# A decoder-layer kernel on one core: the row part of the mLSTM runs as a generator of its own in the second column block of each half

## The chip, the core and the metric

The kernel runs on one core of a Trainium2 chip. The core's engines each take their instructions in order: TensorE (PE in the profile; its weight loads are PEld), VectorE (DVE), ScalarE (ACT), GpSimd (POOL), and SyncE (SP), which in this kernel issues the DMAs. They wait for one another by semaphores. The metric is the time of one execution on the device in microseconds; the kernel before has a median of 2633.44 us over three runs (2632.45 to 2636.21).

## The reference

One layer of a hybrid decoder over 2048 positions of width 1024. A projection feeds three groups of heads: forgetting attention (8 heads), an mLSTM matrix memory (4 heads) and a spatial gating unit (SGU). Cut to what matters here:

```python
p = h @ w_in        # h = RMSNorm(x) * (1 + scale1) + shift1, from mod = silu(c) @ W_ada + b_ada
(q_a, k_a, v_a, q_m, k_m, v_m, o_m, u_s, v_s, f_a, i_m, f_m) = split(p)
F = cumsum(log_sigmoid(f_a))                       # bias of the attention's logits
# mLSTM, chunk by chunk, with the state C, n, m carried on
logf = log_sigmoid(f_m);  bcum = cumsum(logf)
m_t = max(bcum + m, max_s(bcum_t - bcum_s + i_s))
w_intra = exp(bcum_t - bcum_s + i_s - m_t);  w_inter = exp(bcum + m - m_t)
sc = (q k^T) * w_intra
num = w_inter * (q C) + sc v;  den = w_inter * (q n) + sum(sc)
h_out = num / max(|den|, exp(-m_t))
C_new = decay * C + sum_s w_state_s k_s v_s
y_mlstm = sigmoid(o_m) * rms_norm(h_out, g_m_out)
x = x + gate1 * (concat(y_attn, y_mlstm, y_sgu) @ w_out)   # then the ConvFFN
```

The gates' rows (`logf`, `i`, the running maximum `m`, the cumulative sums) are short: 4 heads by 2048 positions. From them come the column factors by which the mLSTM's products are scaled.

## The kernel before

The kernel has a projection stage, then attention, the output projection and the ConvFFN. Only the projection stage (to about 760 us) is touched. It goes twice through seven column blocks of `w_in`, once for each half of the sequence (1024 positions): `steps = [(half, i) ...]`. The blocks of a half are, in order: k of the mLSTM with the gates (`use_km`, i = 0), q and o of the mLSTM with the second half of v's columns (`do_qo`, i = 1), v of the mLSTM (`use_vm`, i = 2), the SGU (`use_sgu`, i = 3), and k, q and v of the attention (`use_qk`, `use_qk`, `use_v`, i = 4 to 6). What the text calls the second block is i = 1.

A block has 8 groups, each one accumulator (`acc`, three of them in PSUM) filled by 24 matmuls: 8 slices of the contraction by the three products `wh hh`, `wl hh`, `wh hl` (L54 to L56), since operands are split into a rounded high and a low part. Then the group is evicted: by ScalarE in `do_qo` (`evq`, L680 and L683) and in `use_km` (L658), by VectorE in `use_vm` (`ev`, L688), by both in `use_qk` (`qsq` on ScalarE, L765, statistics on VectorE, L767, `qn`, L773, and after the transposes `qhi` on ScalarE and `qlo` on VectorE, L786). `use_sgu` has `sy` (L733, L734) and its transposes (L741). The weights of the next block are loaded (`wr`, L582) and split (`wh` by ScalarE, L592; `wl` by VectorE, L593) during a block.

After each group, and in `do_qo` and the other 512-wide blocks once more after its fourth slice, a tick is called. A tick runs callbacks that are due (`after(n, f)`), then one step of each list: `chores`, which in the first half has `rest_of_mod` (each step loads a 128 x 512 piece `wa` of `w_ada` two pieces ahead and adds it into `modacc`, L466 and L468; after eight pieces a row is added, L474), and `background`, whose first generator runs to its next `yield`. So the order in the text is an interleaving by ticks. Each engine's final order comes from a scheduler and may differ from the text, but within an engine it is fixed and executed in order.

`mlstm(qi)` (L852) handles 512 positions, two of them a half. It starts with the row part: the gates are transposed into `psG` (L862, PSUM buffers `mps`), then a chain of VectorE instructions on four rows of 512 (L867 to L887): two scans, the differences, the tile `R` of four row groups (cleared by a memset, L877), `dec`, and a bf16 split of a row in `neb`. The next step makes the attention's cumulative sums `fr` (L891) and stores them to `nf_d`. Three yields later `R` is transposed back (`psR`, L903), and `ecol`, `acol` and `dcol` (L906 to L913) hold the column factors. The rest works per chunk of 128 positions and ends with `yt` (L1038), the mLSTM's output, which is stored to `yt_d`. `yt` shares the tag `sq` (two buffers) with `evq` and `qsq`; `fr` shares `macc` (two) with `modacc`. Tiles of one tag share its buffers: a new one waits until the users of the old one in its buffer are done, stores included.

`mlstm(2*half)` joins `background` in block i = 2 after its fourth group (L690), `mlstm(2*half + 1)` after that block. `log_gates(half)` (L796 to L806) turns the gates into logarithms, two activations (Exp, Ln) with their table loads between four VectorE instructions; the text calls it after block i = 1.

Of the kernel before, what the change touches and what calls it, by code (L numbers as in the profile page):

```python
# [8 lines left out]
F32 = mybir.dt.float32  # L9
F32R = mybir.dt.float32r  # L10
BF16 = mybir.dt.bfloat16
AF = mybir.ActivationFunctionType
ALU = mybir.AluOpType
# [4 lines left out]
P = 128  # L18
# [15 lines left out]
def trunk(  # L34
# [7 lines left out]
    V, A, G, T = nc.vector, nc.scalar, nc.gpsimd, nc.tensor  # L42
# [82 lines left out]
    pool, pp = Mem(), Mem(PSUM)  # L125
# [219 lines left out]
    def down_open_right():  # L345
# [8 lines left out]
        ("wr", 2048, 4), ("wh", 2048, 12), ("wl", 2048, 12), ("st", 8, 4), ("ss", 32, 4),  # L354
    )
    pool.open(
        "proj_r", "right", ("t4k", 4096, 5), ("t2k", 2048, 4), ("macc", 2048, 2), ("sq", 2048, 2), ("tmpA", 512, 2), ("lg", 512, 2), ("fc", 4, 1),
        ("mu", 16, 4), ("wT", 2048, 1), ("gsgu", 1024, 1), ("gbias", 64, 1), ("maskT", 1024, 1),
        ("rmask", 2048, 1), ("sel", 1024, 1), ("selb", 1024, 1), ("neb", 1024, 1), ("dec", 16, 1), ("qz", 2048, 2), ("Cst", 1040, 1), ("mcar", 4, 1), ("ra", 2048, 1), ("rb", 2048, 1),
        ("R", 2048, 1), ("mprev", 20, 2), ("ecol", 1088, 2), ("acol", 64, 2), ("dcol", 32, 2),  # L360
        ("qT", 1024, 2), ("kn", 1024, 2), ("v1", 1040, 2), ("H", 4160, 1), ("kT", 1024, 2), ("M1", 2048, 2),
        ("sc", 2048, 2), ("tm", 1040, 1), ("kw", 1024, 2), ("den", 64, 2), ("nd", 64, 2), ("mss", 64, 2),
# [12 lines left out]
    def misc_ps():  # L375
        return pp.tile([P, 512], F32, name="mp", tag="mp")

    def mps():
        return pp.tile([P, 512], F32, name="mps", tag="mps")
# [241 lines left out]
    background = []  # L621
# [174 lines left out]
    def log_gates(half):  # L796

        g = gates[:, half].rearrange("p a n h -> p (a n h)")
        mn = pool.tile([P, P], F32, name="lg0", tag="lg")
        ab = pool.tile([P, P], F32, name="lg1", tag="lg")  # L800
        V.tensor_scalar(mn, g, 0.0, None, op0=ALU.min)
        V.scalar_tensor_tensor(ab, mn, 2.0, g, op0=ALU.mult, op1=ALU.subtract)
        A.activation(ab, ab, AF.Exp)
        A.activation(ab, ab, AF.Ln, bias=1.0)
        V.tensor_tensor(g[:, 0:64], ab[:, 0:64], mn[:, 0:64], op=ALU.subtract)
        V.tensor_tensor(g[:, 96:P], mn[:, 96:P], ab[:, 96:P], op=ALU.subtract)  # L806


    fc = pool.tile([36, 1], F32, name="fc")
    V.memset(fc, 0.0)  # L810

    rmask = pool.tile([68, 512], F32, name="rmask")[64:68]
# [3 lines left out]
    V.memset(selb, 0.0)  # L816
    for r in (32, 64, 96):
        V.tensor_copy(selb[r : r + 4], bc(ident[r : r + 4, r : r + 4], 2, P))
    neb = pool.tile([P, 512], BF16, name="neb")
    V.memset(neb, 0.0)  # L820

    qzs = [pool.tile([P, 2, 2, P], F32, name="qz%d" % i, tag="qz") for i in range(2)]
    for t in qzs:
# [25 lines left out]
    mcar = pool.tile([68, 1], F32, name="mcar")[64:68]  # L849
    V.memset(mcar, 0.0)  # L850

    def mlstm(qi):  # L852
        t0 = qi * 512
        ra = pool.tile([P, 512], F32, name="ra", tag="ra")
        rb = pool.tile([P, 512], F32, name="rb", tag="rb")
        r4 = lambda t: t.rearrange("p (n l) -> p n l", l=P)
# [4 lines left out]
            o = (qi % 2 * 4 + i) * 4  # L861
            T.transpose(psG[0:100, i * P : (i + 1) * P], g[:, o : o + 100], ident)  # L862
        psI = psG[64:68, :]

        m, e, lf = ra[0:4], ra[32:36], ra[64:68]
        b, a, ne = rb[0:4], rb[32:36], rb[64:68]
        V.tensor_copy(lf, psG[96:100, :])  # L867
        mp_ = pool.tile([36, 5], F32, name="mprev", tag="mprev")[32:36]
        V.tensor_copy(mp_[:, 0:1], mcar)
        V.tensor_tensor_scan(m, lf, psI, mcar, op0=ALU.add, op1=ALU.max)  # L870
        V.tensor_tensor_scan(b, rmask, lf, 0.0, op0=ALU.mult, op1=ALU.add)
        V.tensor_tensor(a, psI, b, op=ALU.subtract)
        V.tensor_tensor(e, m, b, op=ALU.subtract)
        V.tensor_copy(mp_[:, 1:5], r4(m)[:, :, P - 1])
        V.tensor_copy(mcar, mp_[:, 4:5])
        R = pool.tile([P, 512], F32, name="R", tag="R")
        V.memset(R, 0.0)  # L877
        V.tensor_tensor(r4(R[0:4]), bc(mp_[:, 0:4], 2, P), r4(e), op=ALU.subtract)
        V.tensor_scalar(R[32:36], m, -1.0, None, op0=ALU.mult)
        V.tensor_tensor(r4(R[64:68]), r4(a), r4(e)[:, :, P - 1 : P].broadcast_to([4, 4, P]), op=ALU.subtract)  # L880
        V.tensor_copy(R[96:100], a)
        V.tensor_tensor(dec[0:4], mp_[:, 0:4], r4(e)[:, :, P - 1], op=ALU.subtract)

        V.tensor_scalar(neb[32:36], e, -1.0, None, op0=ALU.mult)
        V.scalar_tensor_tensor(ne, e, -1.0, neb[32:36], op0=ALU.mult, op1=ALU.subtract)
        V.tensor_copy(neb[64:68], ne)
        V.tensor_tensor(neb[96:100], ne, neb[64:68], op=ALU.subtract)  # L887
        yield
        fr = pool.tile([P, 512], F32, name="fr", tag="macc")
        for r in (0, 32):  # L890
# [4 lines left out]
            V.tensor_copy(fc[r : r + 4], fr[r : r + 4, 511:512])  # L895
            dma(nf_d[r // 8 : r // 8 + 4, t0 : t0 + 512], fr[r : r + 4])
        yield
        yield
        yield

        psR = mps()
        for i in range(4):
            T.transpose(psR[:, i * P : i * P + 100], R[0:100, i * P : (i + 1) * P], ident[0:100, 0:100])  # L903
        psR4 = psR.rearrange("p (n l) -> p n l", l=P)
        ecol = pool.tile([P, 4, 68], F32, name="ecol", tag="ecol")
        A.activation(ecol, psR4[:, :, 0:68], AF.Exp)  # L906
        acol = pool.tile([P, 4, 4], F32, name="acol", tag="acol")
        V.tensor_copy(acol, psR4[:, :, 96:100])
        psD = mps()
        for pr in range(2):  # L910
            T.matmul(psD[:, pr * 4 : pr * 4 + 4], sel[:, pr, :], dec, start=True, stop=True)
        dcol = pool.tile([P, 2, 4], F32, name="dcol", tag="dcol")
        A.activation(dcol.rearrange("p a b -> p (a b)"), psD[:, 0:8], AF.Exp)  # L913

        H = pool.tile([P, 4, 4, 65], F32, name="H", tag="H")

        got = {}
# [115 lines left out]
        for j in range(2):  # L1033
            yp = mps()
            for n in range(4):
                T.transpose(yp[:, n * P : (n + 1) * P], hq2[:, n, j * P : (j + 1) * P], ident)
            yt = pool.tile([P, 512], F32, name="yt", tag="sq")
            V.scalar_tensor_tensor(yt, yp, gmo[:, j : j + 1], om[:, j, :], op0=ALU.mult, op1=ALU.mult)  # L1038
            dma(yt_d[512 + j * P : 640 + j * P, t0 : t0 + 512], yt)

# [19 lines left out]
    for n, (half, i) in enumerate(steps):  # L1060
        if i == 0:
            make_h(half * 2, x0)
            if half == 0:
                head_setup()
            make_h(half * 2 + 1)
        elif n == nb - 1:
            x0 = [load_x(8 + t) for t in range(4)]
        if n == len(steps) - 1:
            while background:
                if next(background[0], True):  # L1070
                    background.pop(0)
            n_accs[0] = 2
            pool.close("proj_r")
            pp.close("proj_r")
            attention_open_right()

            load_k(0)
            first_rows = [], []
            first = [scores(0, tb, load_q(0, tb, "qA"), r) for tb, r in zip((1, 0), first_rows)]
            load_v(0, (0, 1))  # L1080
            background += first
        nxt[0] = Weights(blocks[steps[n + 1][1]][0]) if n + 1 < len(steps) else None
        blocks[i][1](half, cur)
        started.append(n)
        if nxt[0]:
            nxt[0].cast()
        cur = nxt[0]
        if i == 1:
            log_gates(half)
        if i == 2:  # L1090
            background.append(mlstm(half * 2 + 1))
        if n == nb + 2:
            small_setup()
# [76 lines left out]
    class Block:  # L1170
# [7 lines left out]
        def rows(self, i):  # L1178
            return slice(self.tb * TB + i * P, self.tb * TB + i * P + P)
# [544 lines left out]
```

## Time and profile before

| | us |
|---|---|
| median of 3 runs | 2633.44 (2632.45 to 2636.21) |
| the profiled execution's span | 2631.3 |
| projection stage, first half: second block (i = 1) | 79.0 to 123.6 |
| projection stage, second half: second block | 425.0 to 468.7 |
| TensorE's idle time between 70 and 760, sum | 30.6 |

The median lies 2.1 us above the span of the profiled execution. A row of the timeline has the start and the length in us, the engine, the line, the operation, the tiles written and read with partitions x elements, and in brackets the engine's idle time before it and what ended that. A row of the waits has the waiting engine with tile and line, the arrow to what it waited for, and total us, number and longest.

### The profile page before, as it was taken

To read this page: it belongs to the slowest core of one execution; us is meant where nothing else is said; L and a number is where in the kernel's file an instruction comes from. 1 tells how busy PE (TensorE), PEld (TensorE's weight loads), DVE (VectorE), ACT (ScalarE), POOL (GpSimd) and SP (SyncE) were. 2 spreads that over 40 slices of the span, in tenths; PEclk is the share of its full clock that TensorE was granted. 3 is DMA by queue.
4 is the path that set the end of the run, shared out by engine and by line. 5 is a ranking of instruction groups with operands and counts; after the bars stand their busy time and mean duration, and the time that the engine had idled before them with its cause. 6 is when DMAs were issued, how large, how long until landed. Compare 5 with 4: busy or idle time off the path is not lost.

```text
span 2631.3 us, 36459 instructions
## 1 busy us (share of the span) xinstructions
PE 2539.3 (97%) x12537; PEld 2103.0 (80%) x12537; DVE 2007.0 (76%) x3440; ACT 1269.2 (48%) x2420; POOL 398.9 (15%) x532
## 2 busy tenths in 40 slices
PE   5998999989999999999989999999999999999999
PEld 4886888878787887777868888888888888888787
DVE  7577743565368888866769888888888887898797
ACT  4333343333268888853555444544444444444443
POOL 2012210122336665630000000000000000000000
PEclk9999999999999999999999999999999999999999
DMA  7744653334564355247723222246222226648523
GB/s 244 227 135 131 195 163 107 109 88 121 164 176 116 106 146 149 78 153 238 275 76 104 81 88 80 89 145 232 88 88 81 80 72 247 237 162 302 185 96 116
DMA packets 302592, 379.58 MB, mean 144 GB/s; under 512 B 31934, under 2 KB 194588, under 8 KB 300360
## 3 DMA queue, kind: packets, MB, share of 16 engines
q1 hardware_dynamic: 302408, 377.26, 44.7%
q8 instruction: 99, 1.62, 0.2%
q14 instruction: 85, 0.70, 0.1%
HBM read 276.44 MB, written 100.74 MB: 143 GB/s over the span
## 4 chain that ended last, share of the span: by engine, by line
PE 79%; DVE 11%; DMA 4%; issue 2%; ACT 2%; POOL 1%; SPq 0%; DVEq 0%; ACTq 0%; POOLq 0%
PE ub L56 10%; PE ub L54 10%; PE ub L55 10%; PE acc L54 6%; PE acc L56 6%; PE acc L55 6%; PE db L55 4%; PE db L56 4%; PE db L54 4%; PE sp L206 4%; PE tp L259 3%; PE op L245 2%; PE op L246 2%; DVE wspl L1468 2%; PE wps L56 2%
## 5 line engine op out<-in xcount | busy, mean ns | idle before, releaser
L54 PE MATMUL acc<-wh,hh 128*128 128x512 f32 (+2 forms) x768 | 289.2, 378 | 8.5 <-DVE ev L688 6.6
L54 PE MATMUL ub<-T,wsph 128*128 128x512 f32 x704 | 274.2, 390 | 5.8 <-ACT wsph L1336 5.8
L56 PE MATMUL acc<-wh,hl 128*128 128x512 f32 (+2 forms) x768 | 277.3, 364 | 0.3 <-DVE hl L563 0.3
L55 PE MATMUL acc<-wl,hh 128*128 128x512 f32 (+2 forms) x768 | 277.2, 363 | 0.0
L56 PE MATMUL ub<-T,wspl 128*128 128x512 f32 x704 | 273.7, 389 | 1.7 <-DVE wspl L1337 1.7
L55 PE MATMUL ub<-T,wsph 128*128 128x512 f32 x704 | 273.9, 389 | 0.0
L55 PE MATMUL db<-wspl,wsph 128*128 128x512 f32 x616 | 240.3, 390 | 2.0 <-DVE wspl L1468 1.9
L56 PE MATMUL db<-wsph,wspl 128*128 128x512 f32 x616 | 239.6, 389 | 0.0
L54 PE MATMUL db<-wsph 128*128 128x512 f32 x616 | 238.3, 389 | 0.3 <-ACT wsph L1467 0.3
L1336 ACT CAST wsph<-S 128x512 fp32r<-128x512 f32 x176 | 109.7, 623 | 227.2 <-PE ub L55 157.4
L263 DVE TENSOR_TENSOR plo<-tp,phi 128x512 fp32r<-128x512 f32 (+1 forms) x320 | 186.9, 607 | 31.3 <-ACT phi L262 29.1
L54 PE MATMUL ub<-B,wsph 128*128 128x512 f32 x528 | 207.4, 393 | 2.8 <-ACT wsph L1336 2.8
L56 PE MATMUL ub<-B,wspl 128*128 128x512 f32 x528 | 206.9, 392 | 0.3 <-DVE wspl L1337 0.3
L55 PE MATMUL ub<-B,wsph 128*128 128x512 f32 x528 | 207.0, 392 | 0.0
L223 ACT ACTIVATE L<-L,nm 128x1024 f32<-128x1024 f32 (+2 forms) x192 | 172.6, 902 | 36.0 <-DVE nm L212 34.6
L262 ACT CAST phi<-tp 128x512 fp32r<-128x512 f32 (+1 forms) x320 | 160.0, 521 | 41.1 <-PE tp L259 39.5
L259 PE MATMUL tp<-ident,L 128*128 128x128 f32 x1088 | 177.2, 275 | 2.7 <-POOL L L228 0.9
L206 PE MATMUL sp<-kk,q 128*128 128x512 f32 (+3 forms) x640 | 170.0, 377 | 3.3 <-DVE nm L212 2.2
L54 PEld LDWEIGHTS acc<-wh,hh 128*128 128x128 f32 x768 | 148.3, 193 | 27.9 <-DVE ev L688 6.9
L228 POOL TENSOR_SCALAR L<-L,rs 128x1024 f32<-128x1024 f32 (+2 forms) x192 | 167.3, 881 | 11.0
L1467 ACT CAST wsph<-act 128x512 fp32r<-128x512 f32 x132 | 82.2, 623 | 179.3 <-PE db L55 162.5
L56 PEld LDWEIGHTS acc<-wh,hl 128*128 128x128 f32 x768 | 147.2, 193 | 23.0 <-DVE hl L563 0.8
(340 smaller groups left out, 5934.0 us busy)
## 6 DMA issues: line engine op xcount, KB each, us to landing
w<-in_w_up_dram SPq DMA_DIRECT2D x88, 512.0 KB
wd<-in_w_down_dram SPq DMA_DIRECT2D x176, 256.0 KB
wa<-in_w_ada_dram SPq DMA_DIRECT2D x96, 256.0 KB
act_d<-yc SPq DMA_DIRECT2D x44, 512.0 KB
act<-act_d SPq DMA_DIRECT2D x44, 512.0 KB
wr<-in_w_in_dram SPq DMA_DIRECT2D x64, 256.0 KB
q<-q_d SPq DMA_DIRECT2D x128, 128.0 KB
hc_d<-hl SPq DMA_DIRECT2D x28, 512.0 KB
```

The costliest lines, as they stand in the source:

```text
L54: T.matmul(ps, lh, rh, start=start, stop=False, skip_group_check=resume)
L55: T.matmul(ps, lh, rl, start=False, stop=False, skip_group_check=resume)
L56: T.matmul(ps, ll, rh, start=False, stop=stop, skip_group_check=resume)
L206: T.matmul(sp[:, b : b + bw], q2[n][:, qs], kk[:, s0 + b : s0 + b + bw], start=n == 0, stop=n == 1 and not last)
L223: A.activation(L[c], L[c], AF.Exp, bias=nm[:, n - 1 : n], scale=-1.0, accum_out=rs[:, c : c + 1])
L228: G.tensor_scalar(t, t, rs[:, 0:1], 1.0, op0=ALU.mult, op1=ALU.mult)
L245: T.matmul(op[:, c0:], vv[:, j, :], hi[:, c0:], start=(j == 0), stop=False)
L259: T.transpose(tp[:, i * P : (i + 1) * P], rows[i][j // 8][:, (j % 8) * P : (j % 8 + 1) * P], ident)
L262: A.copy(hi[:, c0:], tp[:, c0:])
L263: V.tensor_tensor(lo[:, c0:], tp[:, c0:], hi[:, c0:].bitcast(F32), op=ALU.subtract)
L1336: A.copy(hi, src)
L1467: A.copy(hi, v)
```

## The change

The row part of `mlstm` becomes a generator `rows(qi)` with steps of its own. Both generators of a half join `background` behind block i = 0, where `log_gates` is now called too, so that they run in block i = 1 one after the other: the gate transposes with the first copies; the two scans; the differences and half of `R`; the rest of `R` and `dec`; `fr`; the transposes back with `psD` (now in a buffer of `misc_ps` instead of `mps`) and the first half of `neb`; and the column factors with the rest of `neb`. `cols[qi]` hands the factors to `mlstm`, which starts with two empty steps. `neb` has two buffers, `R` one that is cleared once at the start. `log_gates` uses the tag `tmpA` instead of `lg`, which is dropped. `yt` takes the buffers `ra` and `rb` instead of `sq`.

```diff
--- before.py
+++ after.py
@@ -354,9 +354,9 @@
         ("wr", 2048, 4), ("wh", 2048, 12), ("wl", 2048, 12), ("st", 8, 4), ("ss", 32, 4),
     )
     pool.open(
-        "proj_r", "right", ("t4k", 4096, 5), ("t2k", 2048, 4), ("macc", 2048, 2), ("sq", 2048, 2), ("tmpA", 512, 2), ("lg", 512, 2), ("fc", 4, 1),
+        "proj_r", "right", ("t4k", 4096, 5), ("t2k", 2048, 4), ("macc", 2048, 2), ("sq", 2048, 2), ("tmpA", 512, 2), ("fc", 4, 1),
         ("mu", 16, 4), ("wT", 2048, 1), ("gsgu", 1024, 1), ("gbias", 64, 1), ("maskT", 1024, 1),
-        ("rmask", 2048, 1), ("sel", 1024, 1), ("selb", 1024, 1), ("neb", 1024, 1), ("dec", 16, 1), ("qz", 2048, 2), ("Cst", 1040, 1), ("mcar", 4, 1), ("ra", 2048, 1), ("rb", 2048, 1),
+        ("rmask", 2048, 1), ("sel", 1024, 1), ("selb", 1024, 1), ("neb", 1024, 2), ("dec", 16, 1), ("qz", 2048, 2), ("Cst", 1040, 1), ("mcar", 4, 1), ("ra", 2048, 1), ("rb", 2048, 1),
         ("R", 2048, 1), ("mprev", 20, 2), ("ecol", 1088, 2), ("acol", 64, 2), ("dcol", 32, 2),
         ("qT", 1024, 2), ("kn", 1024, 2), ("v1", 1040, 2), ("H", 4160, 1), ("kT", 1024, 2), ("M1", 2048, 2),
         ("sc", 2048, 2), ("tm", 1040, 1), ("kw", 1024, 2), ("den", 64, 2), ("nd", 64, 2), ("mss", 64, 2),
@@ -796,8 +796,8 @@
     def log_gates(half):
 
         g = gates[:, half].rearrange("p a n h -> p (a n h)")
-        mn = pool.tile([P, P], F32, name="lg0", tag="lg")
-        ab = pool.tile([P, P], F32, name="lg1", tag="lg")
+        mn = pool.tile([P, P], F32, name="lg0", tag="tmpA")
+        ab = pool.tile([P, P], F32, name="lg1", tag="tmpA")
         V.tensor_scalar(mn, g, 0.0, None, op0=ALU.min)
         V.scalar_tensor_tensor(ab, mn, 2.0, g, op0=ALU.mult, op1=ALU.subtract)
         A.activation(ab, ab, AF.Exp)
@@ -816,8 +816,11 @@
     V.memset(selb, 0.0)
     for r in (32, 64, 96):
         V.tensor_copy(selb[r : r + 4], bc(ident[r : r + 4, r : r + 4], 2, P))
-    neb = pool.tile([P, 512], BF16, name="neb")
-    V.memset(neb, 0.0)
+    nebs = [pool.tile([P, 512], BF16, name="neb%d" % i, tag="neb") for i in range(2)]
+    for t in nebs:
+        V.memset(t, 0.0)
+    R = pool.tile([P, 512], F32, name="R")
+    V.memset(R, 0.0)
 
     qzs = [pool.tile([P, 2, 2, P], F32, name="qz%d" % i, tag="qz") for i in range(2)]
     for t in qzs:
@@ -849,8 +852,11 @@
     mcar = pool.tile([68, 1], F32, name="mcar")[64:68]
     V.memset(mcar, 0.0)
 
-    def mlstm(qi):
+    cols = {}
+
+    def rows(qi):
         t0 = qi * 512
+        neb = nebs[qi % 2]
         ra = pool.tile([P, 512], F32, name="ra", tag="ra")
         rb = pool.tile([P, 512], F32, name="rb", tag="rb")
         r4 = lambda t: t.rearrange("p (n l) -> p n l", l=P)
@@ -861,30 +867,25 @@
             o = (qi % 2 * 4 + i) * 4
             T.transpose(psG[0:100, i * P : (i + 1) * P], g[:, o : o + 100], ident)
         psI = psG[64:68, :]
-
         m, e, lf = ra[0:4], ra[32:36], ra[64:68]
         b, a, ne = rb[0:4], rb[32:36], rb[64:68]
         V.tensor_copy(lf, psG[96:100, :])
         mp_ = pool.tile([36, 5], F32, name="mprev", tag="mprev")[32:36]
         V.tensor_copy(mp_[:, 0:1], mcar)
+        yield
         V.tensor_tensor_scan(m, lf, psI, mcar, op0=ALU.add, op1=ALU.max)
         V.tensor_tensor_scan(b, rmask, lf, 0.0, op0=ALU.mult, op1=ALU.add)
+        V.tensor_copy(mp_[:, 1:5], r4(m)[:, :, P - 1])
+        V.tensor_copy(mcar, mp_[:, 4:5])
+        yield
         V.tensor_tensor(a, psI, b, op=ALU.subtract)
         V.tensor_tensor(e, m, b, op=ALU.subtract)
-        V.tensor_copy(mp_[:, 1:5], r4(m)[:, :, P - 1])
-        V.tensor_copy(mcar, mp_[:, 4:5])
-        R = pool.tile([P, 512], F32, name="R", tag="R")
-        V.memset(R, 0.0)
+        V.tensor_scalar(R[32:36], m, -1.0, None, op0=ALU.mult)
+        V.tensor_copy(R[96:100], a)
+        yield
         V.tensor_tensor(r4(R[0:4]), bc(mp_[:, 0:4], 2, P), r4(e), op=ALU.subtract)
-        V.tensor_scalar(R[32:36], m, -1.0, None, op0=ALU.mult)
         V.tensor_tensor(r4(R[64:68]), r4(a), r4(e)[:, :, P - 1 : P].broadcast_to([4, 4, P]), op=ALU.subtract)
-        V.tensor_copy(R[96:100], a)
         V.tensor_tensor(dec[0:4], mp_[:, 0:4], r4(e)[:, :, P - 1], op=ALU.subtract)
-
-        V.tensor_scalar(neb[32:36], e, -1.0, None, op0=ALU.mult)
-        V.scalar_tensor_tensor(ne, e, -1.0, neb[32:36], op0=ALU.mult, op1=ALU.subtract)
-        V.tensor_copy(neb[64:68], ne)
-        V.tensor_tensor(neb[96:100], ne, neb[64:68], op=ALU.subtract)
         yield
         fr = pool.tile([P, 512], F32, name="fr", tag="macc")
         for r in (0, 32):
@@ -895,23 +896,33 @@
             V.tensor_copy(fc[r : r + 4], fr[r : r + 4, 511:512])
             dma(nf_d[r // 8 : r // 8 + 4, t0 : t0 + 512], fr[r : r + 4])
         yield
-        yield
-        yield
-
         psR = mps()
         for i in range(4):
             T.transpose(psR[:, i * P : i * P + 100], R[0:100, i * P : (i + 1) * P], ident[0:100, 0:100])
+        psD = misc_ps()
+        for pr in range(2):
+            T.matmul(psD[:, pr * 4 : pr * 4 + 4], sel[:, pr, :], dec, start=True, stop=True)
+        V.tensor_scalar(neb[32:36], e, -1.0, None, op0=ALU.mult)
+        V.scalar_tensor_tensor(ne, e, -1.0, neb[32:36], op0=ALU.mult, op1=ALU.subtract)
+        yield
         psR4 = psR.rearrange("p (n l) -> p n l", l=P)
         ecol = pool.tile([P, 4, 68], F32, name="ecol", tag="ecol")
         A.activation(ecol, psR4[:, :, 0:68], AF.Exp)
         acol = pool.tile([P, 4, 4], F32, name="acol", tag="acol")
         V.tensor_copy(acol, psR4[:, :, 96:100])
-        psD = mps()
-        for pr in range(2):
-            T.matmul(psD[:, pr * 4 : pr * 4 + 4], sel[:, pr, :], dec, start=True, stop=True)
         dcol = pool.tile([P, 2, 4], F32, name="dcol", tag="dcol")
         A.activation(dcol.rearrange("p a b -> p (a b)"), psD[:, 0:8], AF.Exp)
-
+        V.tensor_copy(neb[64:68], ne)
+        V.tensor_tensor(neb[96:100], ne, neb[64:68], op=ALU.subtract)
+        cols[qi] = ecol, acol, dcol
+
+    def mlstm(qi):
+        t0 = qi * 512
+        neb = nebs[qi % 2]
+        ecol, acol, dcol = cols[qi]
+
+        yield
+        yield
         H = pool.tile([P, 4, 4, 65], F32, name="H", tag="H")
 
         got = {}
@@ -1034,7 +1045,7 @@
             yp = mps()
             for n in range(4):
                 T.transpose(yp[:, n * P : (n + 1) * P], hq2[:, n, j * P : (j + 1) * P], ident)
-            yt = pool.tile([P, 512], F32, name="yt", tag="sq")
+            yt = pool.tile([P, 512], F32, name="yt", tag=("ra", "rb")[j])
             V.scalar_tensor_tensor(yt, yp, gmo[:, j : j + 1], om[:, j, :], op0=ALU.mult, op1=ALU.mult)
             dma(yt_d[512 + j * P : 640 + j * P, t0 : t0 + 512], yt)
 
@@ -1085,8 +1096,9 @@
         if nxt[0]:
             nxt[0].cast()
         cur = nxt[0]
-        if i == 1:
+        if i == 0:
             log_gates(half)
+            background += [rows(half * 2), rows(half * 2 + 1)]
         if i == 2:
             background.append(mlstm(half * 2 + 1))
         if n == nb + 2:
```

## The prediction

> **What bounds the kernel now.** I read the busy times first, then TensorE's waits, then the timeline around each wait.
>
> ```profile
> span 2631.3 us, 36459 instructions
> PE 2539.3 (97%) x12537; PEld 2103.0 (80%) x12537; DVE 2007.0 (76%) x3440; ACT 1269.2 (48%) x2420; POOL 398.9 (15%) x532
> ```
>
> TensorE is busy 97% of the span, so a change counts only where it alters TensorE's 92 us of idle time, its clock or its instructions. The median of the runs, 2633.4, lies 2.1 above this execution's span; I carry that 2.1 along. TensorE's waits in the projection stage (40 to 760 us), as total, times and longest:
>
> ```profile
> PE trp L781 <- DVE qlo L786: 6.8, 2, 3.4
> PE acc L54 <- DVE ev L688: 6.6, 2, 3.3
> PE mp L741 <- DVE sy L733: 5.9, 2, 3.0
> PE mps L862 <- DVE yt L1038: 4.6, 2, 2.6
> ```
>
> Each occurs twice, once for each half of the sequence; together 23.9 us. All four name VectorE (DVE), and none of the named instructions is long. The timeline says what they queued behind. The first chain of a half, then the second:
>
> ```profile
> 139.37 0.70 DVE L867 COPY ra<-mps 4x512 f32<-4x512 f32 x1
> ...
> 146.25 0.15 DVE L882 TENSOR_TENSOR dec<-mprev,ra 4x4 f32<-4x4 f32 x1
> ...
> 149.04 1.27 DVE L891 TENSOR_TENSOR_SCAN fr<-ones,fc,mps 4x512 f32<-4x512 f32 x1
> ...
> 150.96 0.42 DVE L688 COPY ev<-acc 128x256 f32<-128x256 f32 x1
> 151.44 0.50 PE L54 MATMUL acc<-wh,hh 128*128 128x512 f32 x1 [3.32 <-DVE ev L688]
> ```
>
> ```profile
> 236.26 0.60 ACT L765 ACTIVATE qsq<-acc 128x512 f32<-128x512 f32 x1 [13.56 <-DMA yt_d<-yt]
> 236.53 0.69 DVE L867 COPY ra<-mps 4x512 f32<-4x512 f32 x1
> ...
> 244.92 0.42 DVE L733 TENSOR_TENSOR sy<-mp,gsgu 128x256 f32<-128x256 f32 x1
> ...
> 252.01 0.75 DVE L786 SCALAR_TENSOR_TENSOR qlo<-trp,colA,qhi 128x512 fp32r<-128x512 f32 x1
> ```
>
> From 139.37 on, VectorE works through the row chain on four partitions, and the eviction L688 that frees an accumulator stands behind it until 150.96. The second chain (236.53 on) holds up sy (L733) and qlo (L786) in the same way. The fourth wait is the chain's own start: the gate transposes L862 need the mps buffer that yt (L1038) empties late.
>
> A second cost follows some of these waits. Windows of TensorE alone right behind the gaps (after the matmul count comes the granted clock), with one of all engines first, where the clock is the third value from the end:
>
> ```profile
> 152.00:155.40 3.40, 3.40 (x10) 2.63 (x9) 3.34 (x8) 0.00 (x0) 0.00 (x0) 0.51 0.52 157
> 253.00:256.00 3.00, 3.00 (x18) 0.75 0.79 238
> 496.00:499.00 3.00, 3.00 (x10) 0.64 0.36 106
> 595.00:598.00 3.00, 3.00 (x15) 0.64 0.85 262
> 245.40:248.40 3.00, 3.00 (x15) 1.00 0.23 87
> 587.00:590.00 3.00, 3.00 (x15) 1.00 0.23 87
> 232.00:235.00 3.00, 2.99 (x15) 1.00 0.83 262
> ```
>
> The first four follow the L54 and L781 waits of each half (3.3 to 3.4 us); the clock falls to one half there. At 152.00 it is 0.51 over 3.40 us: 3.40 x 0.49 = 1.7 us of matmul work lost. The last three follow the L741 waits (up to 3.0) and an L862 wait (2.6), with the clock at 1.00. Four dips cost about 4 x 1.7 = 6.8 us.
>
> **The change, part by part.**
>
> *Row chains leave the third and the fifth to sixth column blocks.* Both chains of a half, some 25 instructions each, now run in the second block (do_qo), as steps of two generators. What do VectorE and the PE have there? Block 2 of each half, all engines (PE, PEld, DVE, ACT, POOL):
>
> ```profile
> 79.00:123.60 44.60, 44.60 (x204) 37.06 (x203) 21.75 (x41) 12.68 (x23) 0.00 (x0) 1.00 0.70 231
> 425.00:468.70 43.70, 43.70 (x195) 36.19 (x194) 5.52 (x16) 11.13 (x22) 0.00 (x0) 1.00 0.31 100
> ```
>
> TensorE never idles there, since do_qo is evicted by ScalarE alone (L680, L683): no accumulator waits for VectorE. VectorE has 44.6 - 21.8 = 22.8 us free in the first half, 38.2 in the second. Two chains need at most 2 x (150.96 - 139.37) = 23.2 us with whatever lies among their rows (the chain to dec alone is 146.40 - 139.37 = 7.0). That fits the second half easily, the first only just. Gain where they leave: the waits L781, L54, L741 and L862, 23.9 us, and the four dips, 6.8. Bounds: below, 0 of each wait; above, all. I take all, because nothing else of comparable length stands ahead of those instructions: take the 8.4 us from 236.53 to 244.92 out of the queue, and sy runs before TensorE asks for it at 242.5 (245.40, where the wait ended, less its 2.9). The transposes themselves (L862, L903, L911) are moved, not saved; the PE's instruction count is unchanged.
>
> *log_gates behind block 1.* In the trace it runs there already: the scheduler had hoisted it.
>
> ```profile
> 78.98 0.40 PE L54 MATMUL acc<-hh,wh 128*128 128x512 f32 x1
> 85.78 0.18 DVE L806 TENSOR_TENSOR gates<-lg,lg 128x32 f32<-128x32 f32 x1
> 425.05 0.39 PE L54 MATMUL acc<-hh,wh 128*128 128x512 f32 x1
> 430.22 0.18 DVE L806 TENSOR_TENSOR gates<-lg,lg 128x32 f32<-128x32 f32 x1
> 430.71 0.60 ACT L680 ACTIVATE evq<-acc 128x512 f32<-128x512 f32 x1
> 436.15 0.60 ACT L680 ACTIVATE evq<-acc 128x512 f32<-128x512 f32 x1 [4.84 <-PE acc L56]
> ```
>
> So this edit moves nothing, but it sets when the new chain can start, and that is a *new wait*. In the built order the first gate transposes stand after 22 matmuls of block 2 in the first half, after 12 in the second. A group of 24 takes 436.15 - 430.71 = 5.44, or 0.227 each. TensorE is at them at 78.98 + 22 x 0.227 = 84.0; the gates are ready at 85.96: 2.0 us of waiting. Second half: 425.05 + 12 x 0.227 = 427.8 against 430.40: 2.6. Behind the waiting transposes queue all matmuls of the block, so this is on the path: +4.6. Bounds: 0 (if block 1's tail draws log_gates forward) to 3.4 each with a dip. Both are under the 3.0 that left the clock alone.
>
> [...]
>
> *The later transposes* (L903, now with psD in the misc bank) stand 50 matmuls behind the first ones in the first half, 60 in the second: 11.4 us against a chain of 7.0 plus a weight cast: about 3.6 us to spare. The second chain's have 60 matmuls, about 6 us to spare. Cost 0; without that cover, up to the chain's 7.0.
>
> *Activation tables.* Four more table loads net, all in block 2.
>
> ```profile
> 82.37 1.28 ACT L803 ACT_TABLE_LOAD   x1
> ```
>
> ScalarE idles 4.84 of each 5.44 there, as the row at 436.15 shows, so 4 x 1.28 is covered; uncovered, +5.1.
>
> *Small parts.* One memset of R (L877) in place of four, and a second neb buffer: 0; VectorE has room. yt in ra/rb: the 13.56 us stall of ScalarE at 236.26 came from qsq sharing its buffers with yt's store; it vanishes, and qsq's statistics come sooner. ScalarE was not on TensorE's path there by itself, so 0. The next owner of ra/rb is the next half's row chain, some 100 us later. fr still shares macc with modacc, so the first modacc piece behind each chain waits for two more stores on SP's queue; in the second half there is no modacc left.
>
> *The tight place* is the end of block 2 in the first half. VectorE there has chain one, eight modacc pieces, chain two, eight pieces, then the casts of block 3's last weights. Price of a piece and of the wait for its load:
>
> ```profile
> 107.80 2.33 DVE L468 SCALAR_TENSOR_TENSOR modacc<-wa,cs,modacc 128x512 f32<-128x512 f32 x3
> ...
> 114.28 0.68 DVE L474 TENSOR_TENSOR modacc<-modacc,brow 1x512 f32<-1x512 f32 x1
> ```
>
> ```profile
> 230.56 0.75 DVE modacc L468
> 231.32 2.88 DMA wa<-in_w_ada_dram
> 234.30 0.75 DVE modacc L468
> ```
>
> Seven pieces lie between the first two rows: 0.93 us each. The chain of waits shows the other end: 234.30 - 230.56 = 3.74 a piece when each load is waited for. An estimate at 0.93: VectorE goes from 85.96 through a chain (7.0), fr and its stores (some 4.5), 8 pieces (7.4), the same again, and the row add and four casts (2.4): 126.2, with waits among them 127.4. TensorE ends block 2 at 78.98 + 8 x 5.44 + 2.0 and some 3 us of moved transposes, 127.5, and needs the last weights about 2 us later, 129.4. So 2 us to spare: I take 0 and hold up to 3 us for the range.
>
> **Sum.** 2631.3 - 23.9 - 6.8 + 4.6 = 2605.2 for the span; with the 2.1, 2607.3. Rounded up by 0.2 for the tight place: **2607.5 us**, 26 less than before (1.0%).
>
> **Rivals.**
>
> *A. The second place keeps its waits.* The modacc pieces with their late loads (2.88 above) stand ahead of sy and qlo too. If they and not the chain set those waits, L741 5.9, L781 6.8 and its two dips 3.4 stay: 2607.5 + 16.1 = 2623.6. For it: VectorE is fed by loads there. Against it: in the second half, which has no modacc pieces, the same two waits have the same longest times (3.0 and 3.4, two each).
>
> *B. Slower: VectorE's queue in block 2 of the first half.* 16 pieces stand in order with the chains; loads are issued two ahead of their use, so 14 can be waited for. At 3.74 in place of 0.93 the casts come 14 x 2.81 = 39 us late, less 2 of slack, plus two dips of 1.7: +40.7, 2648. It passes into slower (2638.7) at 14(c - 0.93) - 2 + 3.4 = 31.2, so c = 3.06 us a piece. For it: the chains delay the consumption that triggers each load, and block 2's DMA share is already 0.70. Against it: the stretch at 107.80 in this very block ran at 0.93.
>
> *C. The new waits trip the clock.* Two dips of 1.7: 2611.
>
> *D. The scheduler leaves the chains' work where it hurts,* or each gain returns as a wait of the same size (the transposes after each chain, 7.0 in each of four places, 28 us): 2633 to 2636.
>
> *E. Nothing new waits:* gates ready in time, 2607.5 - 4.6 - 0.2 = 2602.7.
>
> **How the numbers follow.** Forecast 0.58, with its own range 2604 to 2612; E 0.07; C 0.08; A 0.11; B 0.10; D 0.06. Low end 2601 lies under E with room for an unseen gain of 1.7 (one more dip less); the high end 2624 takes in A, and leaves B and D out, 0.16. Under 0.2% (5 us) a measurement of this kernel can hardly tell a change. Faster: 0.58 + 0.07 + 0.08 + 0.11 = 0.84; D is within 0.2%, 0.06; B slower, 0.10.
>
> **What would show it.** The four waits gone from the list, the clock at 1.00 throughout blocks 3 to 6, and qsq's wait for yt_d gone. New: two waits of TensorE for gates (L806's successor), 2.0 and 2.6 us. Wrong by A if the waits for sy and qlo stay in the first half only; by B if TensorE waits in block 2 or at block 3's first weights for wl, or for the accumulators behind a late eviction; by D if the transposes of R wait for the chain.

## The result, and the profile after

The changed kernel takes 2624.97 us (median of 5 runs, 2621.0 to 2626.13) against 2633.44: a ratio of 0.9962 with a 95% interval of 0.9950 to 0.9975. It is faster by 8.5 us, where 26 were forecast, and outside the forecast range (2601 to 2624) by 1 us. The profiled execution has a span of 2624.1, 7.2 below that of before.

TensorE's waits of the projection stage after the change, in the same view as before (total, times, longest):

```profile
PE mps L868 <- DVE gates L806: 5.2, 2, 2.8
PE mp L732 <- DVE sy L733: 4.7, 1, 4.7
PE mp L960 <- DVE sy L733: 3.1, 2, 2.8
PE trp L557 <- ACT h L561: 3.0, 1, 3.0
PE acc L54 <- DVE ev L688: 2.3, 2, 1.3
PE mp L488 <- ACT kT L962: 2.0, 1, 2.0
```

The waits for qlo and yt are gone, as expected, the one for ev has shrunk, and the gate waits are there at nearly the expected size (2.8 and 2.4 for 2.0 and 2.6). But sy has come back at other instructions (L732, the matmul of the SGU's mix, and L960, the transpose of k in the mLSTM), and kT is new. Windows from block 2 of one half to the last transpose before the second half's projection, and from there to the attention's first scores; length, then TensorE busy with its count, and the clock. First the kernel before:

```profile
79.00:412.60 333.60, 317.94 (x1705) 0.99 0.55 168
412.60:698.80 286.20, 273.71 (x1477) 0.99 0.37 109
```

and after the change:

```profile
77.30:414.70 337.40, 321.01 (x1696) 0.98 0.55 167
414.70:694.70 280.00, 274.34 (x1471) 0.98 0.38 111
```

So the account of the 7.2 us is by half: the first half became *longer*, by 3.8, the second shorter by 6.2. Before block 2 it is 1.7 less, behind the projection stage 3.1 less (the rest of the span, 1932.5 to 1929.4), in code that the change does not touch. One execution of each kernel is compared here; the medians differ by 8.5. The clock has its part too. Windows of TensorE behind five waits of the changed kernel:

```profile
85.00:90.00 5.00, 4.72 (x16) 0.66 0.45 136
167.00:171.00 4.00, 4.00 (x14) 0.57 0.40 110
243.00:250.00 7.00, 6.46 (x17) 0.54 0.50 167
433.00:438.00 5.00, 5.00 (x17) 0.66 0.26 72
581.00:588.00 7.00, 6.62 (x24) 0.54 0.07 19
```

Busy time times one minus the clock gives the loss: 1.6, 1.7, 3.0, 1.7 and 3.0 us, 11 in all, against 6.8 before. They stand behind the first gate wait (2.8 us), kT (2.0), sy (4.7), the second gate wait (2.4) and sy again (2.8).

Why is sy late in the first half, with no row chain near it? The chain of waits of the changed kernel ahead of it (start, length, what):

```profile
232.92 0.70 DVE wl L593
...
233.63 0.33 SPq L582
...
234.02 4.40 DMA wa<-in_w_ada_dram
...
238.44 0.76 DVE modacc L468
...
239.22 2.84 DMA wa<-in_w_ada_dram
...
242.15 0.75 DVE modacc L468
242.91 0.66 DVE sy L733 x2
```

sy waits behind modacc pieces, these for their loads, the loads on SP's queue behind a weight load, and that for a cast that runs at 232.92 (the same cast ran at 224.76 before). Casts are late in block 2 already. The last casts of block 3's weights in the timeline of VectorE before the change:

```profile
121.14 0.42 DVE L593 TENSOR_TENSOR wl<-wr,wh 128x256 fp32r<-128x256 f32 x1 [0.26 <-ACT wh L592]
```

and after it, with what stands ahead of them:

```profile
129.21 0.74 DVE L468 SCALAR_TENSOR_TENSOR modacc<-wa,cs,modacc 128x512 f32<-128x512 f32 x1
129.99 0.68 DVE L474 TENSOR_TENSOR modacc<-modacc,brow 1x512 f32<-1x512 f32 x1
130.60 1.41 DVE L593 TENSOR_TENSOR wl<-wr,wh 128x256 fp32r<-128x256 f32 x4
137.50 0.69 DVE L593 TENSOR_TENSOR wl<-wr,wh 128x512 fp32r<-128x512 f32 x1 [5.49 <-ACT wh L592]
```

The casts end at 132.0 instead of 121.6. TensorE itself loses next to nothing there (0.3 us for wl, besides the gate wait of 2.8), but the next block's weights, whose loads wait for these buffers, are cast from 137.5 on (123.1 before), and the evictions ev among them come late: the waits of 1.0 and 1.3 us. So chores of 0.75 us each pass lateness on to the next block through the buffers of the weights. That it runs on from there for 100 us to the cast at 232.92 and to sy is argued, not shown, and run e8 below speaks against it.

In the second half there are no pieces. There sy is late in another way; timeline of the changed kernel:

```profile
577.78 0.41 DVE L733 TENSOR_TENSOR sy<-trp,gsgu 128x256 f32<-128x256 f32 x1
...
580.25 0.69 DVE L773 TENSOR_TENSOR qn<-acc,ss 128x512 f32<-128x512 f32 x1 [1.53 <-POOL ss L128]
580.85 0.41 DVE L733 TENSOR_TENSOR sy<-mp,gsgu 128x256 f32<-128x256 f32 x1
...
581.32 0.69 PE L960 MATMUL mp<-ident,kn 128*128 128x128 f32 x2 [2.83 <-DVE sy L733]
```

L960 is the next mlstm's first transpose, and it wants the buffer mp (in PSUM, as the accumulators are) that sy has yet to empty; sy stands behind qn, which waits for GpSimd. Before the change mlstm began with four yields after its row part, now with two, so L960 comes two ticks earlier, right behind the SGU's mix.

### The profile page after: what moved, and what is told of

It is laid out like the page before. It is cut to its first block, busy times and chain, and to the rows that moved or that the text cites. A ratio compares the mean times of both kernels' runs of the same rounds, so it can differ in the third digit from the quotient of the medians.

```text
span 2624.1 us, 36472 instructions
## 1 busy us (share of the span) xinstructions
PE 2537.4 (97%) x12521; PEld 2101.5 (80%) x12537; DVE 2004.4 (76%) x3438; ACT 1274.2 (49%) x2424; POOL 399.0 (15%) x532
## 4 chain that ended last, share of the span: by engine, by line
PE 76%; DVE 10%; DMA 5%; ACT 3%; issue 3%; POOL 2%; SPq 1%; DVEq 0%; ACTq 0%; POOLq 0%
PE ub L56 10%; PE ub L55 10%; PE ub L54 10%; PE acc L54 5%; PE acc L56 5%; PE acc L55 5%; PE db L55 4%; PE db L56 4%; PE db L54 4%; PE sp L206 3%; PE tp L259 3%; PE wps L55 2%; PE wps L54 2%; PE wps L56 2%; PE op L245 2%
## 5 line engine op out<-in xcount | busy, mean ns | idle before, releaser
L54 PEld LDWEIGHTS acc<-wh,hh 128*128 128x128 f32 x768 | 147.1, 192 | 24.2 <-DVE ev L688 2.7
```

The costliest lines, as they stand in the source:

```text
L54: T.matmul(ps, lh, rh, start=start, stop=False, skip_group_check=resume)
```

## The experiments

The runs came in four groups, each beside runs of the kernel before (medians of 2633.65, 2632.29, 2633.46 and 2632.20). The table gives medians, and ratios to before with their 95% intervals; the changed kernel itself stands at 2624.97, 0.9962 (0.9950 to 0.9975). Against that interval e5 is no different, e1, e2, e4, e7 and e9 overlap it, and e8, e10, e11, e13, e14 and e15 lie at or clear of its edge; differences of 4 to 6 us between single edits are thus no more than likely.

| run | edit | us | ratio |
|---|---|---|---|
| e1 | mlstm with four empty steps | 2618.62 | 0.9942 (0.9927 to 0.9957) |
| e2 | first rows of each half one tick later | 2618.77 | 0.9943 (0.9928 to 0.9958) |
| e3 | yt back in sq | 2637.70 | 1.0017 (1.0007 to 1.0026) |
| e4 | no modacc step in block 2 | 2620.83 | 0.9947 (0.9932 to 0.9962) |
| e5 | no modacc step in the k block | 2624.57 | 0.9965 (0.9955 to 0.9976) |
| e6 | before, with yt in sc | 2631.62 | 0.9998 (0.9988 to 1.0008) |
| e7 | e1, e2 (longer), e5 | 2615.65 | 0.9936 (0.9922 to 0.9951) |
| e8 | e1, e2 (longer), e4 | 2615.01 | 0.9935 (0.9920 to 0.9950) |
| e9 | modacc steps in the second half only | 2626.87 | 0.9976 (0.9967 to 0.9986) |
| e10 | e1, e2 (longer), e9 | 2615.93 | 0.9932 (0.9917 to 0.9947) |
| e11 | e1, e2 (longer), modacc at half rate | 2605.21 | 0.9897 (0.9881 to 0.9914) |
| e12 | before, with modacc at half rate | 2640.86 | 1.0029 (1.0014 to 1.0043) |
| e13 | modacc at half rate, alone | 2611.04 | 0.9915 (0.9900 to 0.9930) |
| e14 | e1, e2 (longer) | 2615.37 | 0.9931 (0.9916 to 0.9946) |
| e15 | e1, modacc at half rate | 2609.73 | 0.9906 (0.9889 to 0.9922) |

**Ticks: e1 and e2.**

```diff
# e1, in mlstm, behind ecol, acol, dcol = cols[qi]
         yield
         yield
+        yield
+        yield
# e2, in rows, behind t0 = qi * 512
+        if qi % 2 == 0:
+            yield
```

> The changed kernel, but mlstm begins with four empty steps instead of two, so that its core keeps the ticks that it had before the change. Theory 1 (crowding: in the first half the 16 modacc pieces and the two row chains share VectorE in block 2, the weights of block 3 are cast and loaded late, and the lateness runs on to sy at 239 us): only the second half's wait L960 <- sy (2.8 us and its clock dip of 3.0) goes, about 2619; the first half's sy wait of 4.7 stays. Theory 2 (position: the core two ticks earlier meets the SGU's mix in the same PSUM buffer): both sy waits go with their dips (4.7 + 3.0 + 2.8 + 3.0 = 13.5), about 2611.5.

> The changed kernel, but the first rows generator of a half begins with one empty step, so that the gate transposes stand 12 matmuls (2.7 us) later. If the two gate waits (2.8 and 2.4 us) and the dips behind them (1.7 each) are a cost of their own, both waits fall below 0.3 us and the time falls by about 8.6, to 2616.4. Rival: the later steps of the chains lose their slack, the transposes of R wait instead and the time stays at 2625, within 2.

e1 came out at 2618.62, as theory 1 had it: the second half's wait at L960 is gone, the first half keeps 3.2 us at L732. e2 took away the second half's gate wait, and 1.0 of the first half's 2.8; in the first half the built order put the transposes after 24 matmuls instead of 22. No transpose of R waits. Each edit is worth about 6 us, less than the 8.6 expected of e2; neither removes the first half's wait for sy (3.2 in e1, 5.3 in e2).

**yt's buffers: e3 and e6.**

```diff
# e3, on the changed kernel
-            yt = pool.tile([P, 512], F32, name="yt", tag=("ra", "rb")[j])
+            yt = pool.tile([P, 512], F32, name="yt", tag="sq")
# e6, on the kernel before
-            yt = pool.tile([P, 512], F32, name="yt", tag="sq")
+            yt = pool.tile([P, 512], F32, name="yt", tag="sc")
```

> The changed kernel with yt back in the sq buffers. By the prediction this part is worth 0 on TensorE: 2625, within 2, with qsq waiting again for the stores of yt. Rival: with the row chains gone, ScalarE's wait is now the next to bind, qsq's accumulators come free late and TensorE waits for them: 5 to 10 us more, 2630 to 2635.

> The kernel before with one change: yt takes the buffers of sc (idle at that point of the chain) instead of sq; the row chains stay where they were. With e3 (row chains moved, yt in sq, 2637.7) this completes a table of two by two. If yt's place and the row chains cost apart from one another, it gains the 12.7 us that lie between e3 and the changed kernel: 2621. If VectorE's row chain holds TensorE up whatever qsq does, yt's place is worth something only once the chain is gone: 2633.6, within 2.5.

The two by two: 2633.4 before, 2631.6 with yt alone moved (no difference that can be measured), 2637.7 with the row chains alone moved (slower), 2625.0 with both. So the edit that I costed at 0 is worth 12.7 us, but only beside the other; e3 itself lies above the 2630 to 2635 of its rival. e3's timeline shows its new stall:

```profile
328.12 0.60 ACT L765 ACTIVATE qsq<-acc 128x512 f32<-128x512 f32 x1 [11.55 <-DMA yt_d<-yt]
...
332.30 1.08 PE L781 MATMUL trp<-ident,qn 128*128 128x128 f32 x4 [4.17 <-DVE qn L773]
```

qsq waits 11.55 us for yt's stores, qn comes late by that, and TensorE waits 4.17 for qn. An earlier stall of qsq for yt (3.4) holds up the copy gr (L484) behind it on ScalarE, for which TensorE waits 2.5. Between 60 and 720 us TensorE waits 6.9 us longer in e3 than in the changed kernel and loses 5.0 more to the clock. And e6's waits show that the row chains hold TensorE whatever qsq does, with one exception: of the two waits for sy, the second half's is gone in this profile.

```profile
PE acc L54 <- DVE ev L688: 6.6, 2, 3.3
PE trp L781 <- DVE qlo L786: 6.3, 2, 3.4
PE mps L862 <- DVE yt L1038: 4.6, 2, 2.7
PE mp L741 <- DVE sy L733: 2.9, 1, 2.9
```

The profiled execution of e6 is the fastest of its ten (2626.84, median 2631.62), so this wait alone says little about the median.

**Where the modacc pieces run: e4, e5, e7, e8 and e14.**

```diff
-        if chores and started and next(chores[0], True):
# e4
+        if chores and len(started) != 1 and started and next(chores[0], True):
# e5
+        if chores and len(started) != 4 and started and next(chores[0], True):
# the longer delay of e7, e8, e10, e11 and e14, in rows, behind t0 = qi * 512
+        for _ in range((2, 0, 1, 0)[qi]):
+            yield
```

> The changed kernel, but the steps of rest_of_mod pause during the second block of the first half and go on from the third, so that no modacc piece stands among the row chains (the 64 pieces end 16 ticks later). Theory 1 (crowding): the first half's waits for ev (1.0 and 1.35), for kT (2.0 and a dip of 1.7) and for sy (4.7 and a dip of 3.0) go, 13.7 in all, about 2611. Theory 2 (position): the sy wait and its dip stay, 6.0 go, about 2619. Rival: the pieces only meet the later blocks instead and the time does not fall, 2625 or more.

> The changed kernel, but the steps of rest_of_mod pause during the k block (the fifth) of the first half and go on after it. If the modacc pieces that stand ahead of sy on VectorE set the first half's wait (4.7 us, and 3.0 of clock behind it), it goes: about 2617. If the tick position alone sets it, or the wait of qn for GpSimd does, at least 2.5 us of it stay and the time is 2621 to 2625.

> The changed kernel with four empty steps in mlstm (e1), the first rows generator begun two ticks later in the first half and one tick later in the second (e2), and no rest_of_mod in the k block (e5). If the causes are separate: e1's 6.3 less, the gate waits and dips 8.6 less, and what e1 left of the sy wait, 3.2 and 1.7: 2625.0 - 6.3 - 8.6 - 4.9 = 2605. Rival: the waits pass from one to the next (later chains push the weight casts of block 3 later), so that less than half of it comes: 2613 or more.

> As e7, but rest_of_mod pauses in the second block instead of the k block. It takes away the crowding in block 2 (the waits for ev, 0.9 and 1.1, for wl, 0.7) and leaves pieces ahead of sy in the k block (3.2 and a dip of 1.7). If the causes are separate: 2625.0 - 6.3 - 8.6 - 2.7 = 2607. If crowding is the root of the late sy as well, below e7, at 2602 or less.

> The two tick repairs of e7 and e8 (four empty steps, later first rows) with the pieces at their full rate in all blocks. If the rate is a cause of its own, the first half keeps a sy wait of 3 and a wait at block 3: 2613 to 2617, as e7 and e8. If the repairs carry e11 alone, 2605 to 2608.

e4 gained 4.1 us, less than theory 1 asked and nearer the 2619 of theory 2: the waits for sy (2.6), ev (1.0 and 1.0) and kT (1.3) are mostly smaller, not gone. e5 gained nothing and decided nothing: a modacc row still stands directly ahead of sy at 243.69, since pieces of the block before are executed there by then, their loads late. e7, e8 and e14 lie within 0.7 us of one another: the tick repairs together are worth 9.6, and neither pause adds anything to them. e7 and e8 thus miss the sums of separate causes (2605 and 2607) by 8 to 11 us, and e14 came in as forecast. A pause moves 16 pieces to a later block, where they crowd as before. In the built order it does not even clear block 2: eight pieces of the block behind run there all the same, from 113.97 on in e4 and from 118.65 in e8, so that neither run is a full test of theory 1. e8 also shows what is enough for the first half's wait for sy. Its casts in block 2 end at 127.3, and the last cast of the k block's weights stands where it stood before the change (224.59 for 224.76); still TensorE waits 3.28 us, for pieces that run directly ahead of sy, behind qn, and do not wait for their loads:

```profile
224.59 0.68 DVE L593 TENSOR_TENSOR wl<-wr,wh 128x512 fp32r<-128x512 f32 x1
...
232.59 2.32 DVE L468 SCALAR_TENSOR_TENSOR modacc<-wa,cs,modacc 128x512 f32<-128x512 f32 x3
234.83 0.42 DVE L733 TENSOR_TENSOR sy<-mp,gsgu 128x256 f32<-128x256 f32 x1
...
235.30 1.22 PE L732 MATMUL mp<-sv,wT 128*128 128x256 f32 x2 [3.28 <-DVE sy L733]
```

So a late cast is not needed for this wait; of the changed kernel's 4.68 us, the 1.4 above 3.28 may come from it.

In e14 TensorE's longest wait is for the vector a (L493) that is made from modacc; a stands behind four late casts of weights, which end at 165.2:

```profile
PE mp L964 <- DVE a L493: 4.9, 1, 4.9
PE mp L732 <- DVE sy L733: 3.5, 2, 3.3
```

**How fast they run: e9 to e13 and e15.**

```diff
-        if chores and started and next(chores[0], True):
# e9, e10
+        if chores and len(started) >= nb and next(chores[0], True):
# e11, e12, e13, e15
+        if chores and started and ticks[0] % 2 and next(chores[0], True):
```

> The changed kernel, but rest_of_mod runs only from the second half on, so that no modacc piece and no load of w_ada is among the blocks of the first half (in e5 pieces of the block before it still stood ahead of sy, so e5 did not decide). If the pieces are what gave the first half its new waits (ev 2.3, kT 2.0, sy 4.7, with dips of 1.7 and 3.0: 13.7), they go and the first half shortens from 337.4 to about 324; the second half gets the pieces and some of these waits. If not, the sy wait of the first half stays above 2.5.

> e9 with the four empty steps of e1 and the later first rows of e2 (two ticks in the first half, one in the second). If crowding by the pieces is a cost only beside the row chains and the SGU of the first half: 2625.0 - 6.3 - 8.6 - 7.6 = 2602.5. If the second half, with the same 64 pieces, builds the same waits: 2610 to 2616, no better than e7.

> The kernel before with nothing changed but a step of rest_of_mod on every other tick. If the row chains alone set its eight waits (23.9), these stay and the time is 2632, within 2.5. If the pieces had a share in them, the first half's waits for yt, sy and qlo (2.6, 2.9, 3.4) shrink and it is 5 to 8 less.

e9 is the clearest attribution, read by half:

```profile
77.30:394.50 317.20, 309.32 (x1667) 0.99 0.43 129
394.50:693.10 298.60, 283.75 (x1518) 0.98 0.54 161
```

Without pieces the first half takes 317.2 in place of 337.4: 11.7 of the 20.2 is matmul time (321.0 - 309.3: the pieces' own matmuls, which moved on, and dips that did not come), 8.5 is waiting. The waits for ev and kT are gone there, and so is L732's 4.7. A wait for sy of 2.8 is left, but at L960, the instruction that waits in the second half of the changed kernel, where no pieces run either; e1 showed that wait to come from the tick position. The second half, now with 64 pieces at the full rate, is 18.6 longer, 9.2 of it waiting, and has the waits that left the first: 4.0 for wl at the end of block 2, 1.7 for kT, 3.4 for sy. So the pieces cost about the same in either half, and the median is no better (2626.87). e10 behaves in the same way (5.5 for wl, 3.3 for sy). e12 excludes that the rate is a gain of its own: the kernel before is 7.4 us *slower* with it, which neither of its two expectations had, and its waits for ev (8.1), sy, qlo and yt remain.

> The repairs of e1 and e2, with a step of rest_of_mod on every other tick, so that its 64 pieces spread over both halves. If it is the rate of the pieces that crowds VectorE and the loads, 2604 to 2608; if a single late piece ahead of sy is enough for the wait, 2612 to 2616 as in e7 and e8.

> The changed kernel with a step of rest_of_mod on every other tick and nothing else. If the rate of the pieces is the main cause of the first half's new waits (11.3 with their dips of 4.7), these go and the gate waits (5.2, dips 3.4) and the second half's L960 wait (2.8, dip 3.0) stay: 2625.0 - 12 = 2613. If the pieces alone are not the cause and the tick positions are, 2620 or more.

> The half rate with the four empty steps, but the rows begin as in the changed kernel, so that TensorE waits for the gates in both halves. If the gate waits are a cost of their own, this stands above e11 by 5 to 8.6 (5.2 of waiting and up to 3.4 of clock): 2610 to 2614. If they are made up for later, 2605 to 2608.

The rate alone, on the changed kernel, brings 13.9 us (e13), and with both tick repairs the time is 2605.21 (e11), the fastest here: 28 us below before. It is not that the loads come in time at this rate: in the first half (77 to 400 us) the pieces of e13 still wait 12.0 us for theirs, those of the changed kernel 14.2. What changes is where they stand: between 218 and 240 us, around sy, VectorE runs no piece in e13 or e11, and block 2's last cast ends at 125.5 in e13 (132.0 in the changed kernel). Whether it is the lower rate as such, or the places that the built order gives the pieces at that rate, these runs do not separate. e11's longest waits, and its two halves:

```profile
PE mp L964 <- ACT kT L966: 2.2, 1, 2.2
PE trp L557 <- DVE xt L520: 1.6, 4, 0.9
```

```profile
77.30:396.30 319.00, 312.52 (x1704) 1.00 0.54 162
396.30:670.00 273.70, 272.62 (x1484) 1.00 0.45 131
```

Both halves are short now, at a clock of 1.00. e15, with the gate waits left in, stands 4.5 above e11, by ratio only 2.4, and the intervals overlap; its profile has gate waits of 1.4 and 1.9 and no dip. What the gate waits cost beside the half rate stays open.

## Why the prediction was wrong

**What held.** The bound and the cause of the eight waits: with the chains gone from VectorE's queue, the waits for qlo and yt vanish, in e3 too, where yt stays in sq. e6 shows that yt's place had not set them, but for one wait for sy, and e12 that the rate of the pieces had not. log_gates was already in place. The gate waits came as worked out (5.2 for 4.6), and e2 takes one of them away. The later transposes and the table loads cost nothing that a wait shows. And the gain of 26 can be had: e11 has it, with the chains still in the second block, begun a tick or two later.

**The sum.** For the span 26.1 us were forecast and 7.2 came, 18.9 less. In the two halves TensorE still waits 22.1 us; the forecast left 8.9 of the 28.2 before. The clock loses 11.0 there; the forecast left nothing. That is 24.2 in all, of which the stretches outside the halves give back 4.8. So the largest misses are the clock (11.0) and the waits for sy (4.7 and 3.1).

**The step that failed** is the sentence "I take all, because nothing else of comparable length stands ahead of those instructions". In the first half something does: the modacc pieces. Once the chain is gone, TensorE waits 4.7 us for sy behind them, 2.3 for ev and 2.0 for kT; without pieces in that half (e9) these three waits are gone, and at half their rate (e13), where no piece stands ahead of sy, too; a wait of 2.8 at L960 is there in both instead, by the tick position. Rival A named the pieces at that place, with 2623.6, close to the 2625 measured. That closeness is luck: the waits that A kept, for sy at L741 and for qlo at L781, are both gone, and other terms make up the time. A's argument against itself (the second half has the same waits without pieces) was true of the kernel before and said nothing about what comes next once the chain is gone.

The end of block 2 was mis-sized as well. VectorE's last cast there ends at 132.0, 10 us later than before and 4.6 later than the estimate of 127.4. The queue is the one of rival B, but its price is another: eight pieces took 8.8 and 8.2 us, about 1.05 each and far from B's 3.74, where I had 7.4; the two chains with fr and what lies among their rows took 13.4 and 13.5, where I had 11.5. I had called 2 us of slack enough and did not cost what a late end does to the next block (ev, 2.3 us).

**A term mis-sized at zero**: yt's place. "ScalarE was not on TensorE's path there by itself, so 0." By itself, true (e6). Once the chains are gone it is on the path, and worth 12.7 us (e3).

**A term left out**: mlstm's two empty steps where there had been more. I counted matmuls up to the row transposes, but not the new position of the core's first transposes against the SGU's: 2.8 us and a dip of 3.0 in the second half (removed in e1).

**The clock.** "Both are under the 3.0 that left the clock alone": the profiled run dips behind waits of 2.8, 2.4 and 2.0. Rival C, with 0.08, was part of the truth: its two dips behind the gate waits came at the size that it gave (1.6 and 1.7). But it is no matter of the wait's size alone. Behind the 2.0 stand eight matmuls of one column and six short ones, so that no product of 512 columns starts from 162.5 to 167.1:

```profile
165.31 1.05 PE L488 MATMUL mp<-ones,modacc 128*128 128x1 f32 x8 [1.97 <-ACT kT L962]
```

Whether these short matmuls have a part in the dip was not tested. At the same place e4 loses 1.7 us behind a wait of only 1.3. And in e13 there are two waits of 2.82 and 2.83 at the same instruction, with the same instructions around them, one in each half; windows right behind them:

```profile
231.60:235.60 4.00, 4.00 (x13) 0.63 0.10 33
565.50:569.50 4.00, 3.95 (x24) 1.00 0.12 33
```

The same wait costs 1.7 us of clock in one half (1.5 of it within the first of these windows) and nothing in the other; in the changed kernel the wait of 2.83 at this instruction cost 3.0, in e4 1.7.

**Left open.** The wait for h at the border of the halves is 3.0 against 1.9 before and between 1.4 and 3.2 in the other runs; no run isolates it. The 3.1 us behind the projection stage belong to the clock: in windows of 1 us the profile before loses 9.4 us there to lower clocks, the one after 4.2, while TensorE waits 1.1 longer. Why the dips differ in code that is the same, and whether the clock also makes the spread of the runs (2621.0 to 2626.1), was not tested. The 1.7 us before block 2 have no explanation. That e12 is slower than the kernel before was measured, not explained: between 60 and 720 us its profile shows 3.7 us more of waiting and 4.2 more lost to the clock. What decides whether a wait of 2 to 3 us is followed by a dip stays open.

## What to carry to other kernels

When a wait is taken from a queue, look up what else stands ahead of the instruction that waited: the next in line sets the gain, and an edit that is worth nothing alone (yt's place) may decide the sign of another (e3 is slower than before). Work moved under a busy block competes with the chores already there; the two repairs that paid were to spread the chores (a step every other tick, 14 us) and to shift the moved work by a tick or two against its neighbours (9.6). A pause that only pushes the chores to a later block gained 4.1 at most, and nothing beside the other repair.

## What was not expected of the hardware

Waits well under 3 us (2.4 and 2.8 for the gates, 2.0 for kT with short matmuls behind it) were followed by a stretch at half the clock (0.50 in windows of 1 us) with 1.6 to 1.7 us lost, while 3.0 us in the kernel before (L741, the clock at 1.00 behind it) was followed by none. One and the same wait of 2.8 us at L960 lost 3.0 (the changed kernel), 1.7 (e4, and the first half of e13) or nothing (the second half of e13) behind it. For this kernel, 97% busy on TensorE, an estimate from these figures (2.83 us of waiting with 3.0 of clock behind it) is that a wait between 2 and 3 us may cost up to about as much again.
